# Loading the second round of scores into the staging space ahead of the first batch's gathers, in an argmax-gather-scatter kernel

## The chip, the cores and the metric

The kernel runs on one core of a Trainium2 chip. The metric is the device time of one execution in microseconds (us); lower is better. Before the change three runs took 908.44 to 910.4 us, with a median of 910.17 us.

## The reference

```python
def setup_inputs():
    B, S, H = (8, 2048, 2560)
    return {'scores': np.random.randn(B, S, S).astype(np.float32), 'values': np.random.randn(B, S, H).astype(np.float32)}

def reference(scores, values):
    best_j = np.argmax(scores, axis=2)
    b_idx = np.arange(B)[:, None]
    gathered = values[b_idx, best_j, :].copy()
    out = np.zeros_like(values)
    np.add.at(out, (b_idx, best_j, slice(None)), gathered)
    return out
```

For each of 8 batches, every one of the 2048 rows of scores picks the column with its maximum. Row j of the output is row j of the values times the number of score rows that picked j. So a values row that nobody picked becomes zeros, one that was picked once is copied, and one that was picked several times is multiplied by its count. With random scores a row is picked 0 times, once, or several times with chances of about 0.368, 0.368 and 0.264.

## The kernel before

**Scores.** `count_steps` (line 150) goes through the 16 tiles of a batch, 128 score rows each. A score load (line 160, queue of SyncE, called SP in the profile) brings two tiles at once: 128 partitions x 4096 numbers, 2 MiB, from 64 loads in all. This document numbers the loads 0 to 63 as the variable `x` does; batch 0 has loads 0 to 7, batch 1 loads 8 to 15. For each tile VectorE (DVE) runs MAX8 (line 168) and FIND_INDEX8 (line 169); every four tiles it makes one-hot matrices (lines 174 to 184), from which TensorE adds the counts of the batch into `cnt_ps` (line 187). After each tile the generator yields.

**Where the scores land.** There are ten places of 2 MiB. Seven are the buffers of the pool `spool` (`s_tile`). The other three lie in `vbig`, a tensor of six staging slots of 2560 columns (10,240 bytes per partition, one values row each) that the gathers use later. The test on line 155 sends loads 0, 1, 2 and 10, 11, 12 into `vbig`, at columns 0 to 4095, 4096 to 8191 and 8192 to 12287; all others go to `s_tile`. Loads 10, 11 and 12 belong to tiles 4 to 9 of batch 1. They overlay slots 0 to 4.

**Values.** `value_steps` (line 191) turns the counts of a batch into three kinds of transfers, all issued by GpSimd (POOL) as indirect DMAs whose index lists hold an out-of-range number where a row is to be skipped:

- a copy (`copy_once`, line 203, issued on line 33): rows that were picked once, from values to output directly, 16 per batch;
- a zero scatter (`scatter` of `zrow`, line 139): rows of zeros for the rows that nobody picked, 7 per batch;
- for the many-counted rows a gather (line 134) into a slot of `vbig`, a multiplication by the counts on ScalarE (ACT, line 280), and a scatter to the output (line 139), 5 of each per batch. The gathers take slots in turn (`stage`, line 145): batch 0 uses slots 0 to 4, batch 1 slots 5, 0, 1, 2, 3.

The index lists come from VectorE work between the yields: the scans (lines 212 to 228), the large one-hot compare `oh` (line 239), and, after two matmul groups (lines 258 and 261), the lists `many_i` and `zero_i` and the factors `many_c` (lines 268 to 272).

**What sets the order.** PE, DVE, ACT and SP run in the order in which the program is written (line 300). GpSimd's DMAs are placed by the scheduler, which keeps dependences. The framework derives waits from program order: whoever comes later in the program and touches a place that an earlier instruction reads or writes must wait for that one. The outer loop (line 302) runs the steps of batch b+1's counting and advances `value_steps` of batch b by one step after each tile. Batch 0 is the exception: on lines 309 to 311 its `value_steps` are run to their end before batch 1's counting begins. So in program order batch 0's gathers and scatters, which use slots 0 to 4, come before loads 10, 11 and 12, which overwrite these slots.

The end of the program (line 321) waits until all copies and zero scatters have landed.

Of the kernel before, what the change touches and what calls it, by code (L numbers as in the profile page):

```python
# [36 lines left out]
def kernel(  # L37
# [8 lines left out]
    _, _, H = values.shape  # L46
# [144 lines left out]
    def value_steps(b, cnt_ps):  # L191
# [98 lines left out]
                    copy_once(rest.pop(0))  # L290


        for part in (zeros, gathers) if b == 0 else (gathers, zeros):
            part()
        for k in range(MCAP):
            scatter(staged[k], mi[:, k:k + 1])
        yield
# [2 lines left out]
    with tc.manual_schedule(engines={ET.PE, ET.DVE, ET.Activation, ET.SP}):  # L300
        pending = iter(())
        for b in range(B):
            cnt_ps = psum_c.tile([P, NT], FP32)
            for _ in count_steps(b, cnt_ps):
                next(pending, None)
            for _ in pending:
                pass
            pending = value_steps(b, cnt_ps)
            if b == 0:
                for _ in pending:  # L310
                    pass
        for _ in pending:
            pass
        over = fin.tile([1, 2], FP32)
        nc.vector.tensor_single_scalar(out=over[:, 0:1], in_=totmax[0:1, 0:1], scalar=float(ZCAP * P), op=ALU.is_gt)
        nc.vector.tensor_single_scalar(out=over[:, 1:2], in_=totmax[0:1, 1:2], scalar=float(MCAP * P), op=ALU.is_gt)
        over_i = fin.tile([1, 1], INT32)
        nc.vector.tensor_tensor(out=over_i[:], in0=over[:, 0:1], in1=over[:, 1:2], op=ALU.add)
# [44 lines left out]
```

## Time and profile before

| | us |
|---|---|
| three runs, median (lowest to highest) | 910.17 (908.44 to 910.4) |
| the profiled execution, device time | 909.32 |
| its span, first to last instruction | 907.4 |
| VectorE busy | 687.8 |
| GpSimd busy (issuing DMAs) | 275.7 |
| ScalarE busy | 102.9 |
| TensorE busy | 18.0 |

The profile is one execution on the chip. A line of the timeline gives the start in us, the duration, the engine, the line of the program, the operation, what it writes and reads, how many, and in brackets how long the engine was idle before it and what ended that wait. A line of the waits gives who waited for whom: the total in us, how often, and the longest. A line of the stretches view gives for a piece of the span (from:to) its length, the busy time of PE, PEld, DVE, ACT and POOL with the number of instructions in brackets, the clock of TensorE, the mean busy share of the core's 16 DMA engines, and the GB/s that they moved. The first of the DMA queues, `q0`, is GpSimd's; `q1` is that of SP, with the score loads. In all 347.05 MB are moved.

### The profile page before, as it was taken

The numbers are of one execution on the slowest core, as the hardware profiler recorded it, in microseconds if no ns is written. First come the engines' busy times: TensorE is split into PE (matmuls) and PEld (weight loads), VectorE is DVE, ScalarE is ACT, GpSimd is POOL, SyncE is SP. The second block draws the span as 40 slices with busy tenths as digits, with TensorE's granted clock in tenths as the row PEclk, the third lists the DMA queues.
The fourth block names the chain that finished last, engine by engine and source line by source line (L and its number), as shares of the span: only waits on it lengthen the run. The fifth ranks groups of instructions, "written<-read, shape, count | busy, mean of one in ns | idle before, by whom it ended". The sixth has DMA issues, their size and how long they took to land.

```text
span 907.4 us, 2251 instructions
## 1 busy us (share of the span) xinstructions
PE 18.0 (2%) x400; PEld 16.9 (2%) x400; DVE 687.8 (76%) x741; ACT 102.9 (11%) x43; POOL 275.7 (30%) x275
## 2 busy tenths in 40 slices
PE   0000000000000000000000000000000000000000
PEld 0000000000000000000000000000000000000000
DVE  6999820499999999999999999999999994000000
ACT  2000005000023000032000320002200320400500
POOL 0001742000456012623015430064211753735600
DMA  9920899999779999999999999999999999999991
GB/s 381 428 116 12 260 401 424 373 428 381 286 304 417 426 426 429 427 426 424 429 427 424 429 427 426 427 427 426 428 429 418 423 425 423 423 424 421 424 399 53
DMA packets 47249, 347.05 MB, mean 382 GB/s; under 512 B 18279, under 2 KB 18279, under 8 KB 18279
## 3 DMA queue, kind: packets, MB, share of 16 engines
q0 software_dynamic: 38016, 212.67, 57.0%
q1 hardware_dynamic: 9216, 134.22, 35.1%
q14 instruction: 14, 0.11, 0.0%
q8 instruction: 3, 0.05, 0.0%
HBM read 354.42 MB, written 293.60 MB: 714 GB/s over the span
## 4 chain that ended last, share of the span: by engine, by line
DVE 68%; DMA 11%; POOL 9%; issue 7%; POOLq 0%; PE 0%; SPq 0%; DVEq 0%
DVE am L169 30%; DVE mx L168 28%; DMA out_dram<-vbig,many_i 9%; POOL out_dram L33 5%; POOL out_dram L139 3%; DVE oh L239 3%; DMA vbig<-in_scores_dram 2%; DVE oh_lo L178 2%; POOL vbig L134 1%; DVE lo L174 1%; DVE oh_hi L182 0%; DVE rz L247 0%; DVE hi L176 0%; DVE ez L243 0%; DVE rank L233 0%
## 5 line engine op out<-in xcount | busy, mean ns | idle before, releaser
L169 DVE FIND_INDEX8 am<-mx,s_tile 128x8 uint32<-128x2048 f32 x116 | 265.0, 2285 | 0.0
L168 DVE MAX8 mx<-s_tile 128x8 f32<-128x2048 f32 x116 | 264.3, 2278 | 0.0
L33 POOL DMA_INDIRECT out_dram<-in_values_dram,ones_i x128 | 134.7, 1052 | 228.6 <-DVE m L214 190.4
L280 ACT ACTIVATE vbig<-vbig,many_c 128x2560 f32<-128x2560 f32 x40 | 96.7, 2426 | 755.9 <-DMA vbig<-in_values_dram,many_i 748.6
L134 POOL DMA_INDIRECT vbig<-in_values_dram,many_i x40 | 42.1, 1052 | 228.3 <-DMA out_dram<-vbig,many_i 193.0
L139 POOL DMA_INDIRECT out_dram<-vbig,many_i x40 | 39.0, 976 | 110.6 <-ACT vbig L280 104.6
L168 DVE MAX8 mx<-vbig 128x8 f32<-128x2048 f32 x12 | 27.4, 2280 | 58.0 <-DMA vbig<-in_scores_dram 58.0
L139 POOL DMA_INDIRECT out_dram<-zrow,zero_i x56 | 58.5, 1045 | 17.1 <-issue 16.1
L239 DVE TENSOR_TENSOR oh<-lo,fill_f 128x4096 f16<-128x4096 uint32 x8 | 35.4, 4428 | 0.0
L169 DVE FIND_INDEX8 am<-mx,vbig 128x8 uint32<-128x2048 f32 x12 | 27.4, 2285 | 0.0
L178 DVE TENSOR_TENSOR oh_lo<-lo,lane_f 128x512 bf16<-128x512 uint32 x32 | 22.2, 694 | 0.4
L187 PE MATMUL cnt_ps<-oh_hi,oh_lo 128*128 128x16 bf16 x128 | 8.1, 174 | 622.9 <-DVE oh_hi L182 581.4
L187 PEld LDWEIGHTS <-oh_lo 128*128 128x128 bf16 x128 | 8.4, 105 | 622.6 <-DVE oh_lo L178 599.3
L169 DVE MATCH_VALUE_LOAD am<-mx,s_tile 128x8 f32 x116 | 10.7, 92 | 4.0
L182 DVE TENSOR_TENSOR oh_hi<-hi,lane_f 128x64 bf16<-128x64 uint32 x32 | 7.0, 219 | 0.0
L174 DVE TENSOR_SCALAR lo<-am 128x4 uint32<-128x4 uint32 x32 | 6.0, 186 | 1.1
L258 PE MATMUL m_ps<-rm,oh 128*128 128x16 f16 x128 | 4.7, 175 | 81.0 <-DVE rm L254 81.0
L176 DVE TENSOR_SCALAR hi<-am 128x4 uint32<-128x4 uint32 x32 | 5.7, 177 | 0.0
L258 PEld LDWEIGHTS <-oh 128*128 128x128 f16 x128 | 4.1, 105 | 81.6 <-DVE rm L254 74.8
L261 PE MATMUL z_ps<-rz,oh 128*128 128x16 f16 x128 | 4.6, 174 | 0.0
L261 PEld LDWEIGHTS <-oh 128*128 128x128 f16 x128 | 4.0, 104 | 0.0
L247 DVE TENSOR_TENSOR rz<-ez,row_f 128x256 f16<-128x256 f16 x8 | 3.4, 429 | 0.3
(52 smaller groups left out, 55.0 us busy)
## 6 DMA issues: line engine op xcount, KB each, us to landing
s_tile<-in_scores_dram SPq DMA_DIRECT2D x58, 2048.0 KB, 12.0
vbig<-in_scores_dram SPq DMA_DIRECT2D x6, 2048.0 KB, 9.1
out_dram<-in_values_dram,ones_i POOLq DMA_INDIRECT x128
out_dram<-zrow,zero_i POOLq DMA_INDIRECT x56
vbig<-in_values_dram,many_i POOLq DMA_INDIRECT x40
out_dram<-vbig,many_i POOLq DMA_INDIRECT x40
```

What stands on the lines that cost most here:

```text
L33: return eng.add_instruction(ins)
L134: nc.gpsimd.indirect_dma_start(out=v, out_offset=None, in_=values_flat[:, :], in_offset=bass.IndirectOffsetOnAxis(ap=idx, axis=0), bounds_ ...
L139: note(nc.gpsimd.indirect_dma_start(out=out_flat[:, :], out_offset=bass.IndirectOffsetOnAxis(ap=idx, axis=0), in_=v, in_offset=None, bound ...
L168: nc.vector.max(out=mx[:], in_=rows)
L169: nc.vector.max_index(out=am[:, g, :], in_max=mx[:], in_values=rows)
L174: nc.vector.tensor_single_scalar(out=lo[:], in_=am[:, :, 0], scalar=P - 1, op=ALU.bitwise_and)
L178: nc.vector.tensor_tensor(out=oh_lo[:], in0=lo[:].unsqueeze(2).to_broadcast([P, G, P]), in1=lane_f[:].unsqueeze(1).to_broadcast([P, G, P]) ...
L187: nc.tensor.matmul(out=cnt_ps[:], lhsT=oh_lo[:, g, :], rhs=oh_hi[:, g, :], start=(t == 0), stop=(t == NT - 1))
L239: nc.vector.tensor_tensor(out=oh[:], in0=lo[:].unsqueeze(2).to_broadcast([P, 2 * NT, P]), in1=fill_f[:].unsqueeze(1).to_broadcast([P, 2 * ...
L258: nc.tensor.matmul(out=m_ps[:], lhsT=oh[:, NT + t, :], rhs=rm[:, t, :, :].rearrange("p a k -> p (a k)"), start=(t == 0), stop=(t == NT - 1))
L261: nc.tensor.matmul(out=z_ps[:], lhsT=oh[:, t, :], rhs=rz[:, t, :], start=(t == 0), stop=(t == NT - 1))
L280: nc.scalar.activation(out=v, in_=v, func=mybir.ActivationFunctionType.Copy, bias=0.0, scale=mc[:, k:k + 1])
```

## The change

Batch 0's `value_steps` are no longer run to their end before batch 1's counting. Only their first four steps are: the last of these issues the zero scatters and then stops at the first of ten new yields. The other nine yields are passed one per tile of batch 1, and after tile 9 of batch 1 the gathers, the multiplications and the scatters of batch 0 follow. By then loads 10, 11 and 12 (and all loads up to those of tile 9) have been written down. So in program order these three loads now come before batch 0's gathers. Other batches keep their order of parts.

```diff
@@ -290,8 +290,15 @@ value_steps
-        for part in (zeros, gathers) if b == 0 else (gathers, zeros):
-            part()
+        if b == 0:
+            zeros()
+
+            for _ in range(10):
+                yield
+            gathers()
+        else:
+            gathers()
+            zeros()
         for k in range(MCAP):
             scatter(staged[k], mi[:, k:k + 1])
         yield
@@ -307,8 +314,8 @@ the outer loop
             pending = value_steps(b, cnt_ps)
             if b == 0:
-                for _ in pending:
-                    pass
+                for _ in range(4):
+                    next(pending)
```

SP's queue around loads 8 to 13, with what each waits for: names that begin with DMAHW are score loads, DMASW are GpSimd's DMAs. Before:

```order
L160 DMA s_tile<-in_scores_dram 128x4096 [waits DMAHW0_49]
L160 DMA s_tile<-in_scores_dram 128x4096 [waits DMAHW1_49]
L160 DMA vbig<-in_scores_dram 128x4096 [waits DMASW6_49,DMASW5_49,DMAHW2_49,DVE_49,Activation_49]
L160 DMA vbig<-in_scores_dram 128x4096 [waits DMASW7_49,DMASW0_49,DMAHW3_49,DVE_49,Activation_49]
L160 DMA vbig<-in_scores_dram 128x4096 [waits DMASW1_49,DMAHW4_49,DVE_49,Activation_49]
L160 DMA s_tile<-in_scores_dram 128x4096 [waits DMAHW5_49,DVE_49]
```

And now, at the same place of SP's queue:

```order
L160 DMA s_tile<-in_scores_dram 128x4096 [waits DMAHW0_49]
L160 DMA s_tile<-in_scores_dram 128x4096 [waits DMAHW1_49]
L160 DMA vbig<-in_scores_dram 128x4096 [waits DMAHW2_49,DVE_49]
L160 DMA vbig<-in_scores_dram 128x4096 [waits DMAHW3_49,DVE_49]
L160 DMA vbig<-in_scores_dram 128x4096 [waits DMAHW4_49,DVE_49]
L160 DMA s_tile<-in_scores_dram 128x4096 [waits DMAHW5_49,DVE_49]
```

The three loads keep their place in the queue; their waits for GpSimd's DMAs (batch 0's scatters) and for ScalarE are gone, and the waits for an earlier load and for VectorE stay.

GpSimd's queue from batch 0's last zero scatters to batch 1's gathers, as one piece of the difference (batch 0's five gathers, its five scatters, then batch 1's copies and gathers):

```order
 L139 DMA out_dram<-zrow,zero_i 16384x2560 x6
-L134 DMA vbig<-in_values_dram,many_i 128x2560 [waits DMAHW0_49]
-L134 DMA vbig<-in_values_dram,many_i 128x2560 [waits DMAHW1_49]
-L134 DMA vbig<-in_values_dram,many_i 128x2560
-L134 DMA vbig<-in_values_dram,many_i 128x2560 [waits DMAHW2_49]
-L134 DMA vbig<-in_values_dram,many_i 128x2560 [waits Activation_49]
+L134 DMA vbig<-in_values_dram,many_i 128x2560 [waits DMAHW2_49,DVE_49]
+L134 DMA vbig<-in_values_dram,many_i 128x2560 [waits DMAHW3_49,DVE_49]
+L134 DMA vbig<-in_values_dram,many_i 128x2560 [waits DVE_49]
+L134 DMA vbig<-in_values_dram,many_i 128x2560 [waits DMAHW4_49,DVE_49]
+L134 DMA vbig<-in_values_dram,many_i 128x2560 [waits DVE_49,Activation_49]
```

The gathers stand at the same place in GpSimd's queue, but each now waits for VectorE too, which must have read the scores of loads 10 to 12 from that slot. A little further on, where batch 1's transfers begin:

```order
-L33 DMA out_dram<-in_values_dram,ones_i 16384x2560 [waits landed0,DVE_49]
-L33 DMA out_dram<-in_values_dram,ones_i 16384x2560 x5
+L33 DMA out_dram<-in_values_dram,ones_i 16384x2560 [waits DVE_49]
+L33 DMA out_dram<-in_values_dram,ones_i 16384x2560 x3
 L134 DMA vbig<-in_values_dram,many_i 128x2560 [waits DMASW2_49,DVE_49]
```

Batch 1 has four copies ahead of its first gather now, where it had six, and the wait for batch 0's copies and zeros (`landed0`) has moved from here to the end of the program, where the other batches' stand.

## The prediction

> **What bounds the kernel now.** I read the page first: the span, and the GB/s that the DMA engines moved in 40 slices of 22.7 us.
>
> ```profile
> span 907.4 us, 2251 instructions
> GB/s 381 428 116 12 260 401 424 373 428 381 286 304 417 426 426 429 427 426 424 429 427 424 429 427 426 427 427 426 428 429 418 423 425 423 423 424 421 424 399 53
> ```
>
> The DMA engines run at one level, about 426 GB/s, for nearly the whole span. The exceptions are a hole in the third to fifth slice and a second, shallower one in the tenth to twelfth. A kernel that is otherwise held by its transfers gets shorter by what such holes are worth, so the question is who makes them. The waits name it:
>
> ```profile
> DVE mx L168 <- DMA vbig<-in_scores_dram: 58.0, 2, 52.1
> ```
>
> ```profile
> SPq L160 <- DMA out_dram<-vbig,many_i: 156.2, 3, 145.4
> ```
>
> VectorE waits once for 52.1 us, for a score load into `vbig`; and the SP queue sat 145.4 us before that load, waiting for scatters out of `vbig`. The timeline of SP shows the place:
>
> ```profile
> 0.75 1.33 SPq L160 DMA_DIRECT2D vbig<-in_scores_dram  x3
> 2.12 11.50 SPq L160 DMA_DIRECT2D s_tile<-in_scores_dram  x7
> 159.17 12.00 SPq L160 DMA_DIRECT2D vbig<-in_scores_dram  x3
> 171.28 84.47 SPq L160 DMA_DIRECT2D s_tile<-in_scores_dram  x12
> ```
>
> Ten loads are issued by 13.6 us, the eleventh (load 10) at 159.17. Everything behind it on SP waits too. GpSimd's timeline tells what it waits for (first copy of batch 0; first and last gather; first and last scatter; then batch 1's first copy and first gather):
>
> ```profile
> 87.77 1.12 POOL L33 DMA_INDIRECT out_dram<-in_values_dram,ones_i  x1 [85.81 <-DVE m L214]
> ...
> 121.85 1.04 POOL L134 DMA_INDIRECT vbig<-in_values_dram,many_i  x1 [0.30 <-issue]
> ...
> 127.09 0.99 POOL L134 DMA_INDIRECT vbig<-in_values_dram,many_i  x1 [0.30 <-issue]
> ...
> 144.69 1.00 POOL L139 DMA_INDIRECT out_dram<-vbig,many_i  x1 [16.61 <-ACT vbig L280]
> ...
> 156.61 0.96 POOL L139 DMA_INDIRECT out_dram<-vbig,many_i  x1 [1.35 <-ACT vbig L280]
> ...
> 234.43 0.98 POOL L33 DMA_INDIRECT out_dram<-in_values_dram,ones_i  x1 [76.85 <-DVE m L214]
> ...
> 257.00 1.04 POOL L134 DMA_INDIRECT vbig<-in_values_dram,many_i  x1 [11.48 <-DVE empty L270]
> ```
>
> Load 10 needs batch 0 counted (88 us), copied, zeroed, gathered, scaled and scattered. On VectorE:
>
> ```profile
> 8.43 2.29 DVE L168 MAX8 mx<-vbig 128x8 f32<-128x2048 f32 x1 [5.91 <-DMA vbig<-in_scores_dram]
> ...
> 82.91 2.28 DVE L169 FIND_INDEX8 am<-mx,s_tile 128x8 uint32<-128x2048 f32 x1
> ...
> 98.61 2.28 DVE L168 MAX8 mx<-s_tile 128x8 f32<-128x2048 f32 x1
> ...
> 170.38 2.29 DVE L168 MAX8 mx<-vbig 128x8 f32<-128x2048 f32 x1 [52.08 <-DMA vbig<-in_scores_dram]
> ...
> 228.77 2.29 DVE L168 MAX8 mx<-s_tile 128x8 f32<-128x2048 f32 x1
> ...
> 759.75 0.15 DVE L318 TENSOR_TENSOR over_i<-over 1x1 int32<-1x1 f32 x1
> ```
>
> Batch 0's 16 tiles take 8.43 to 85.2, or 9.6 us per load of two tiles. From 170.38 to 228.77 lie twelve tiles, 9.73 us per load. VectorE has its last result at 759.75, but the span goes on to 907.4. The stretches view shows why:
>
> ```profile
> 10.00:50.00 40.00, 0.51 (x8) 0.52 (x8) 39.62 (x35) 0.00 (x0) 0.00 (x0) 1.00 1.01 431
> 50.00:86.00 36.00, 0.25 (x4) 0.26 (x4) 35.65 (x29) 0.00 (x0) 0.00 (x0) 1.00 0.04 17
> 86.00:95.00 9.00, 0.45 (x6) 0.50 (x7) 8.38 (x24) 0.00 (x0) 6.62 (x3) 1.00 0.17 48
> 95.00:112.00 17.00, 1.00 (x32) 0.90 (x31) 14.04 (x15) 0.00 (x0) 13.04 (x14) 1.00 0.96 311
> 112.00:160.00 48.00, 0.26 (x4) 0.26 (x4) 6.21 (x8) 12.03 (x5) 17.31 (x18) 1.00 1.01 410
> 160.00:172.00 12.00, 0.00 (x0) 0.00 (x0) 1.62 (x1) 0.00 (x0) 0.00 (x0) 1.00 0.83 323
> 172.00:214.00 42.00, 0.51 (x8) 0.53 (x8) 41.62 (x36) 0.00 (x0) 0.00 (x0) 1.00 1.00 428
> 214.00:234.00 20.00, 0.25 (x4) 0.26 (x4) 19.69 (x20) 0.00 (x0) 0.00 (x0) 1.00 0.83 319
> 234.00:260.00 26.00, 1.49 (x38) 1.32 (x38) 25.59 (x40) 0.00 (x0) 11.96 (x9) 1.00 0.67 239
> 260.00:300.00 40.00, 0.51 (x8) 0.52 (x8) 39.65 (x33) 12.14 (x5) 24.21 (x25) 1.00 1.01 420
> 300.00:760.00 460.00, 12.75 (x288) 11.86 (x288) 452.83 (x499) 48.34 (x20) 142.16 (x138) 1.00 1.01 426
> 760.00:880.00 120.00, 0.00 (x0) 0.00 (x0) 0.00 (x0) 24.16 (x10) 59.06 (x60) 1.00 1.02 423
> 880.00:907.40 27.40, 0.00 (x0) 0.00 (x0) 0.00 (x0) 0.00 (x0) 0.00 (x0) 1.00 0.23 97
> ```
>
> From 260 to 880 the DMA engines are full (share 1.01), through VectorE's end at 760. After 760 they still carry 120 x 423 and 27.4 x 97 GB/s-us, 53.4 MB, about two batches of values. So the bound is the DMA engines from 260 on; VectorE never waits there, it runs ahead of a backlog. What decides the end is how many bytes were moved before the saturated part begins.
>
> **The change part by part.** *The holes, added up.* From 50 to 260 the rows above move 0.6 + 0.4 + 5.3 + 19.7 + 3.9 + 18.0 + 6.4 + 6.2 = 60.5 MB. At 426 GB/s this is 142 us of work in 210 us: **68 us** are lost, by stretch 34.6 (50:86), 8.0, 4.6, 1.8, 2.9, 0, 5.0 and 11.4 (234:260).
>
> That rate is weighed against a rule. The row 300:760 holds 426 GB/s for 460 us. The Trainium skill, page HBM Reference, section Specifications (TRN2), gives an effective share of about 358 GB/s per core, and about 425 for a core that streams alone. By 358 the 60.5 MB would be 169 us of work, the loss 41, and the time below some 27 us higher; the trace agrees with the page's other figure.
>
> *What is removed.* Load 10 now waits only for load 2 and for VectorE to be done with load 0, which is at 8.43 + 9.6 = 18 us; loads 11 and 12 at 28 and 37. All three are issued while the first ten still move (to about 51.4: the row 50:86 has 0.6 MB left, 1.4 us). A load is 2.097 MB, 4.92 us at 426. So 10 to 12 land by 66.2. Loads 13 to 17 are issued as VectorE frees loads 3 to 7: at 46.8, 56.4, 66.0, 75.6, 85.2. They land by 71.1, 76.0, 80.9, 85.9 and, for the last, about 93: the first load of all came 7.7 us after its issue (0.75 to 8.43), 2.8 more than its bytes need. VectorE's stall of 52.1 goes too: at 118.3 load 10 has long been there. All its later work comes 52.1 earlier, batch 1's first copy at 182.3 for 234.43, its gathers at 204.9 for 257.00, its last result at 707.7.
>
> *What is kept of the holes.*
> - 50:86: 34.6 before; the transfers now follow one another almost without a gap. I keep 1.5 (0 to 3).
> - 86:95: 8.0 before; load 17 gives 4.9 of the 9 us, the first copy 1.0 as before. I keep 3 (0 to 8.0).
> - 95:112: only copies, 311 GB/s; load 18 comes at 108.3 (98.61 + 9.7). 4.6 before; I keep 3.5 (2 to 4.6).
> - 112:160, 1.8 before: I keep 1, since a load every 9.7 us joins. 160:172: nothing, load 10 no longer starts from an empty queue.
> - 214:260, 16.4 before, falls at 162 to 208 now. GpSimd's transfers are these:
>
> ```profile
> q0 software_dynamic: 38016, 212.67, 57.0%
> ```
>
> 212.67 MB over 8 batches is 26.6 MB each, 62 us at 426. From 95 to 182 there are 61 us of batch 0's transfers, eight loads (18 to 25, issued 108 to 176) of 4.92 = 39, and 4.5 of slow copying: 105 us of work in 87. So the engines stay full, and about 18 us are left over at 182. From 182 to 205 four copies (0.48 MB each, 6 us at the row's 311 GB/s) and load 26 come in, with the start of load 27 about 12 us: 30 for 23. That covers it, but not by much, and the last scatters wait for ScalarE one by one. I keep 4, between 0 and the 11.4 of before, nearer the full end because a backlog exists now and did not then.
>
> Kept: 1.5 + 3 + 3.5 + 1 + 4 = 13. **Gain 68 - 13 = 55 us.**
>
> *What is added.* Batch 0's gathers wait for VectorE to finish loads 10 to 12. VectorE is done with load 10 at 118.3 + 9.7 = 128, 11 at 138, 12 at 147.5; GpSimd gets to the first gather at 121.85 and holds there. Its gathers go at 128, 138, 138, 147.5, 147.5 instead of 121.85 to 127.09. Behind them on GpSimd are only batch 0's scatters and then batch 1's copies, not ready until 182.3. The scatters came 17.6 to 29.5 us after the last gather was issued (144.69 and 156.61 against 127.09), so now by about 177. Cost on the path: 0, while batch 1's copies are the cover; without it, 20.4 us (147.5 - 127.09) at most. Two copies fewer ahead of batch 1's gathers is counted above; `landed0` at the end costs nothing, batch 0 having landed long before. Ten more yields issue nothing.
>
> **The sum.** Profiled execution 909.32 - 55 = 854.3. The runs' median is 0.85 above that execution, so **855**.
>
> **The rivals.**
> 1. *The second hole comes back.* Between batch 1's copies and gathers the engines run dry as before (11.4 for 4), and the load into 86:95 starts late (8.0 for 3). Kept 13 + 7.4 + 5 = 25, gain 43: 867; with the first alone 862.5. For it: only four copies now stand ahead of the gathers. Against: 18 us of backlog at 182. Chance 0.12.
> 2. *VectorE paces the end.* If the tail behind VectorE's last result (907.4 - 759.75 = 147.6) were a fixed chain, the gain would be the stall alone, 52.1: 858. Against it: the tail is 53.4 MB at full rate. Chance 0.1, within the range.
> 3. *Memory itself is the limit, no change.* The page counts
>
> ```profile
> DMA packets 47249, 347.05 MB, mean 382 GB/s; under 512 B 18279, under 2 KB 18279, under 8 KB 18279
> ...
> HBM read 354.42 MB, written 293.60 MB: 714 GB/s over the span
> ```
>
> If the memory could give no more than this mean, filling holes would only slow the rest, and 648 MB would again take 907 us. Against it: the mean includes 36 us at 17 GB/s, and 347.05 MB moved stand for 648 in memory, so the 426 of 300:760 is 795 already. The Trainium skill, HBM Reference, same section, gives about 716 GB/s per memory domain, by which 648 MB need 905 us, no gain; the 795 speaks against it as a cap on this count. Chance 0.03.
> 4. *Slower: GpSimd stands still behind the late gathers.* If batch 0's scatters landed after batch 1's gathers want their slots (204.9), GpSimd, in order, would hold those and all copies and zeros behind them. It costs when the last scatter lands after 205, and makes the kernel slower when it lands after about 262 (57 us later, more than the gain); at 270 the time would be 918 or so. How long gather and scatter take with full engines is seen near the end (a gather, its scatter, the gather that waits for that to land):
>
> ```profile
> 739.78 1.04 POOL L134 DMA_INDIRECT vbig<-in_values_dram,many_i  x1 [0.30 <-issue]
> ...
> 789.83 0.98 POOL L139 DMA_INDIRECT out_dram<-vbig,many_i  x1 [0.30 <-issue]
> ...
> 822.21 1.02 POOL L134 DMA_INDIRECT vbig<-in_values_dram,many_i  x1 [17.36 <-DMA out_dram<-vbig,many_i]
> ```
>
> 50 and 32 us: 147.5 + 82 is 230, still 32 us short of 262, and the loads would fill the engines meanwhile. Chance 0.02.
>
> That load 10 isn't freed is excluded by SP's order: no wait for a scatter is left on it.
>
> **How the numbers follow.** My forecast has 0.73, its own range 848 (kept 6, the 55 becoming 62) to 862 (kept 20). Rival 2 lies inside; of rival 1 the range takes most, up to 866. So 848 to 866. About 0.2% is what a measurement of this kernel can tell from no change: faster 0.95, same 0.03, slower 0.02.
>
> **What would show it.** SP issues loads 10 to 12 before 40 us; VectorE has no wait above 5 us after its start and ends near 708; the stretch 50 to 86 runs above 400 GB/s; GpSimd waits for VectorE before batch 0's gathers until 147; from 112 on the engines are full except for a dent below 5 us near 190 to 205. The prediction is wrong if that dent is as deep as before, if VectorE waits for scores again, or if the saturated level sinks below 420 GB/s.

## The result and the profile after

| | before | after |
|---|---|---|
| runs, median (lowest to highest), us | 910.09 (908.44 to 910.4) | 860.15 (860.01 to 860.97) |
| the profiled execution, us | 909.32 | 860.97 |
| its span, us | 907.4 | 859.2 |

Before has one run more here than the three given ahead, so its median moves from 910.17 to 910.09. The ratio of the times is 0.9457, with a 95% interval of 0.944 to 0.9473: the kernel is 49.9 us faster. 855 had been predicted, with a range of 848 to 866.

The page of the changed kernel gives the span and the GB/s in 40 slices, of 21.5 us each:

```profile
span 859.2 us, 2246 instructions
GB/s 378 427 427 427 289 390 428 419 413 248 428 419 426 427 426 429 426 429 424 427 426 428 425 427 428 429 426 425 428 424 420 424 426 413 425 425 421 425 370 35
```

The deep hole is gone: the second to fourth slices are at 427. Two dents remain: the fifth slice (289) and the tenth (248). VectorE's waits, and SP's timeline:

```profile
DVE mx L168 <- DMA vbig<-in_scores_dram: 6.2, 1, 6.2
```

```profile
0.75 1.33 SPq L160 DMA_DIRECT2D vbig<-in_scores_dram  x3
2.12 11.81 SPq L160 DMA_DIRECT2D s_tile<-in_scores_dram  x7
18.57 19.23 SPq L160 DMA_DIRECT2D vbig<-in_scores_dram  x3
...
108.13 9.51 SPq L160 DMA_DIRECT2D s_tile<-in_scores_dram  x2
...
156.49 0.33 SPq L160 DMA_DIRECT2D s_tile<-in_scores_dram  x1
...
166.74 9.51 SPq L160 DMA_DIRECT2D s_tile<-in_scores_dram  x2
...
187.86 0.33 SPq L160 DMA_DIRECT2D s_tile<-in_scores_dram  x1
```

VectorE waits for scores at the start alone, for the first load. Loads 10 to 12 are issued from 18.57 to 37.8. The rows further down matter for the error below: loads 18 and 19 from 108.13, load 20 only at 156.49, 21 and 22 from 166.74, 23 at 187.86. GpSimd's first gather and its last scatter of batch 0, then batch 1's first copy and first gather:

```profile
128.05 1.04 POOL L134 DMA_INDIRECT vbig<-in_values_dram,many_i  x1 [6.22 <-DMA s_tile<-in_scores_dram]
...
170.17 0.96 POOL L139 DMA_INDIRECT out_dram<-vbig,many_i  x1 [3.52 <-ACT vbig L280]
182.61 0.98 POOL L33 DMA_INDIRECT out_dram<-in_values_dram,ones_i  x1 [11.48 <-DVE m L214]
...
205.19 1.04 POOL L134 DMA_INDIRECT vbig<-in_values_dram,many_i  x1 [17.77 <-DVE empty L270]
```

The first gather is later (128.05 for 121.85), as the added wait says. The view names a score load as what ended its wait, but it lies behind VectorE's last read of load 10, which in VectorE's timeline starts at 125.50 and takes 2.29 us. Batch 1's copies are not held up by this: GpSimd is idle for 11.48 us before them. The stretches view (last two columns: share of the DMA engines, GB/s) answers the table of before:

```profile
50.00:86.00 36.00, 0.26 (x4) 0.27 (x4) 35.65 (x30) 0.00 (x0) 0.00 (x0) 1.00 1.00 423
86.00:95.00 9.00, 0.45 (x6) 0.49 (x7) 8.38 (x23) 0.00 (x0) 6.34 (x2) 1.00 0.78 285
95.00:112.00 17.00, 1.00 (x32) 0.90 (x31) 14.13 (x16) 0.00 (x0) 13.01 (x14) 1.00 0.94 309
112.00:182.00 70.00, 1.01 (x16) 1.04 (x16) 69.25 (x62) 12.14 (x5) 17.57 (x18) 1.00 1.01 418
182.00:190.00 8.00, 0.21 (x2) 0.13 (x2) 7.83 (x18) 0.00 (x0) 3.89 (x4) 1.00 1.00 394
190.00:202.00 12.00, 1.02 (x32) 0.93 (x32) 11.86 (x12) 0.00 (x0) 0.00 (x0) 1.00 0.57 228
202.00:205.00 3.00, 0.26 (x4) 0.26 (x4) 2.93 (x8) 0.00 (x0) 0.00 (x0) 1.00 0.38 71
205.00:210.00 5.00, 0.00 (x0) 0.00 (x0) 4.93 (x6) 0.00 (x0) 3.90 (x4) 1.00 0.86 349
210.00:260.00 50.00, 0.52 (x8) 0.53 (x8) 49.59 (x39) 12.14 (x5) 24.68 (x26) 1.00 1.01 424
260.00:700.00 440.00, 11.75 (x256) 10.96 (x256) 433.98 (x476) 48.45 (x20) 142.05 (x138) 1.00 1.01 426
```

A stretch of length L that moved r GB/s lost L x (426 - r) / 426. The rows give 0.3, 3.0, 4.7, 1.3, then 0.6 + 5.6 + 2.5 + 0.9 = 9.6 from 182 to 210, and 0.2: together 19 us, where the kernel before lost 68. The difference, 49, is the 48.2 us between the two spans within 1 us. VectorE's last result comes at

```profile
707.95 0.15 DVE L325 TENSOR_TENSOR over_i<-over 1x1 int32<-1x1 f32 x1
```

### The profile page after: what moved, and what is told of

The parts are those of the page before. It is cut to its first block, busy times and chain, and to the rows that moved or that the text cites. A ratio compares the mean times of both kernels' runs of the same rounds, so it can differ in the third digit from the quotient of the medians.

```text
span 859.2 us, 2246 instructions
## 1 busy us (share of the span) xinstructions
PE 18.0 (2%) x400; PEld 17.0 (2%) x400; DVE 687.9 (80%) x741; ACT 103.2 (12%) x43; POOL 271.7 (32%) x275
## 3 DMA queue, kind: packets, MB, share of 16 engines
HBM read 354.42 MB, written 293.60 MB: 754 GB/s over the span
## 4 chain that ended last, share of the span: by engine, by line
DVE 69%; DMA 9%; POOL 7%; issue 5%; another core or an unknown queue 4%; PE 0%; POOLq 0%
DVE am L169 31%; DVE mx L168 29%; DMA out_dram<-vbig,many_i 8%; DVE oh L239 3%; POOL out_dram L33 3%; POOL out_dram L139 3%; DVE oh_lo L178 2%; POOL vbig L134 1%; DMA vbig<-in_scores_dram 1%; DVE lo L174 1%; DVE oh_hi L182 0%; DVE rz L247 0%; DVE hi L176 0%; DVE ez L243 0%
## 5 line engine op out<-in xcount | busy, mean ns | idle before, releaser
L33 POOL DMA_INDIRECT out_dram<-in_values_dram,ones_i x128 | 130.1, 1016 | 155.3 <-DVE m L214 117.0
L139 POOL DMA_INDIRECT out_dram<-vbig,many_i x40 | 41.4, 1035 | 105.8 <-ACT vbig L280 101.1
```

The source lines that it names most:

```text
L33: return eng.add_instruction(ins)
L139: note(nc.gpsimd.indirect_dma_start(out=out_flat[:, :], out_offset=bass.IndirectOffsetOnAxis(ap=idx, axis=0), in_=v, in_offset=None, bound ...
```

## The experiments

Theory A, that of the prediction: the DMA engines set the end, and what decides is how much they have moved before the part from about 210 us on, in which they stay full until near the end. Theory B (rival 2 of the prediction): VectorE's end plus a fixed tail sets it. Times are medians; the ratio to the kernel before, measured together with it, and the interval of this ratio stand beside each. In this section *batch 1's early copies* are those ahead of its first gather.

### Does the dent cost what the sum says? More early copies

```diff
-        first = NT if b == 0 else 4
+        first = NT if b < 2 else 4
```

> The changed kernel with all 16 copies of batch 1 (instead of 4) ahead of its first gather. Theory A (the end is set by how many bytes the DMA engines have moved; the changed kernel runs dry from 190 to 205 us because nothing is queued there): twelve more copies of 0.48 MB are about 13 us of work, the dent of some 9.6 us closes, 851 us (849 to 854), while VectorE's last result stays at 708. Theory B (VectorE's end plus a fixed tail sets the time): VectorE's end doesn't move, so 860.

Measured: **852.98 us** (0.9381, 0.9369 to 0.9394), 7.2 us faster than the changed kernel, within A's bounds. The stretches from 182 on:

```profile
182.00:190.00 8.00, 0.22 (x2) 0.13 (x2) 7.86 (x17) 0.00 (x0) 6.17 (x6) 1.00 1.02 392
190.00:202.00 12.00, 1.02 (x32) 0.93 (x32) 11.86 (x12) 0.00 (x0) 9.86 (x8) 1.00 1.00 403
202.00:205.00 3.00, 0.26 (x4) 0.26 (x4) 2.87 (x9) 0.00 (x0) 2.39 (x3) 1.00 0.99 345
205.00:210.00 5.00, 0.00 (x0) 0.00 (x0) 4.97 (x6) 0.00 (x0) 3.78 (x5) 1.00 1.04 352
```

The dent is filled to 392 to 403 GB/s; these rows still lose 0.6 + 0.6 + 0.6 + 0.9 = 2.7 us, 6.9 less than the 9.6 of the changed kernel and close to the gain of 7.2. VectorE's last result:

```profile
711.09 0.15 DVE L325 TENSOR_TENSOR over_i<-over 1x1 int32<-1x1 f32 x1
```

It came 3 us *later* than in the changed kernel (VectorE waited 3.31 us on line 270 shortly before it), while the end came 8.7 us of span earlier. That excludes B.

### Fewer early copies

```diff
-        first = NT if b == 0 else 4
+        first = NT if b == 0 else 0 if b == 1 else 4
```

> The changed kernel with none of batch 1's copies (instead of 4) ahead of its first gather. Theory A (bytes moved by the DMA engines before the saturated part): four copies of 0.48 MB, 1.13 us each at 426 GB/s, leave the stretch 182 to 205 us, the dent gets 4.5 us deeper, 864.7 us (862 to 867). Theory B (VectorE's end plus a fixed tail): 860.

Measured: **859.64 us** (0.945, 0.9437 to 0.9463), neither slower than the changed kernel nor the 864.7 expected. The edit did something that its expectation doesn't say: there are only twelve places for copies beside the gathers and the zero scatters, so this kernel leaves four of batch 1's copies out and its output lacks their rows. It has 4.5 us less to move and a dent that is deeper by about as much. The time of a kernel with less work cannot judge the theory, so the same was run with the four copies after the zero scatters:

```diff
+        while rest:
+            copy_once(rest.pop(0))
         for k in range(MCAP):
             scatter(staged[k], mi[:, k:k + 1])
```

> The changed kernel with none of batch 1's copies ahead of its first gather (instead of 4), and all 16 of them issued: five between the gathers, seven between the zero scatters, the last four after these. The run before this one of that kind had left these four copies out and took 859.64 us. Theory A (bytes moved before the saturated part begins at 205 us): the same dry stretch, and now four copies of 1.13 us more to move after it, 864.2 us (863 to 866). Rival (the four copies ahead of the gathers matter for nothing): 860.

Measured: **862.43 us** (0.9484, 0.947 to 0.9497). 2.3 us slower than the changed kernel, about half of what A expects, just below its 863 to 866, and clear of the rival's 860. Its trace shows the deeper dent, and a second difference:

```profile
190.00:202.00 12.00, 1.02 (x32) 0.93 (x32) 11.83 (x15) 0.00 (x0) 0.00 (x0) 1.00 0.19 78
...
202.00:205.00 3.00, 0.25 (x4) 0.26 (x4) 2.93 (x8) 0.00 (x0) 1.91 (x2) 1.00 0.93 284
```

```profile
202.78 1.04 POOL L134 DMA_INDIRECT vbig<-in_values_dram,many_i  x1 [30.87 <-DVE empty L270]
```

The engines fall to 78 GB/s as they should, but the gather that ends the dent comes at 202.78, 2.4 us sooner than in the changed kernel. Most of this comes from batch 0: between the two instructions of line 270 VectorE waited 1.8 us in the changed kernel and doesn't here. That wait is in the traces of before, of the changed kernel and of some experiments, and absent from others; the hardware section takes it up. With 2.4 us added back, which is an estimate and was not measured, the run would stand at 864.8, near the 864.2 expected.

### Is VectorE's end on the path?

```diff
                 nc.vector.max_index(out=am[:, g, :], in_max=mx[:], in_values=rows)
+                if b == 4 and u < 4:
+                    again = small.tile([P, 8], FP32, name="again")
+                    nc.vector.max(out=again[:], in_=rows)
```

> The changed kernel with eight more MAX8 of 2.28 us on VectorE, whose results are not used, in the first eight tiles of batch 4: 18 us of extra VectorE work in the saturated part. Theory A (the DMA engines set the end from about 205 us on, VectorE runs ahead of a backlog): VectorE's last result comes at 726, the time stays 860 (859 to 863). Theory B (VectorE paces the end): 878.

Measured: **860.25 us** (0.9458, 0.9443 to 0.9472), the time of the changed kernel. VectorE's last result:

```profile
727.86 0.15 DVE L328 TENSOR_TENSOR over_i<-over 1x1 int32<-1x1 f32 x1
```

It moved by 20 us and the end by none. So the 51.8 us by which the change ended VectorE's work sooner (707.95 for 759.75) are not themselves the gain.

### One of the three loads left behind

```diff
-            for _ in range(10):
+            for _ in range(8):
                 yield
```

> The changed kernel with eight yields instead of ten: batch 0's gathers come after tile 7 in program order, so loads 10 and 11 precede them and load 12 comes after and waits for two scatters. Theory A (what counts is how long SP's queue is blocked, and with it every load behind): loads 12 to 17 aren't there by 95 us, VectorE stalls about 40 us before tile 8 of batch 1, most of the gain is lost, 897 us (885 to 905). Rival (the gain comes load by load, a third for each of the three): 877.

Measured: **892.48 us** (0.9813, 0.9798 to 0.9828). Two loads of three in front keep 17 of 50 us; a third for each load would have kept 33. SP's waits and VectorE's:

```profile
SPq L160 <- DMA out_dram<-vbig,many_i: 137.7, 1, 137.7
```

```profile
DVE mx L168 <- DMA vbig<-in_scores_dram: 41.2, 2, 35.1
```

SP is blocked for 137.7 us by load 12 alone, as it was for 145.4 by load 10 before, and VectorE stalls for 35.1 (52.1 before). From 50 to 86 most of the hole is back:

```profile
50.00:86.00 36.00, 0.26 (x4) 0.27 (x4) 35.65 (x29) 0.00 (x0) 0.00 (x0) 1.00 0.31 133
```

The row loses 24.8 us, where before lost 34.6: the difference, 9.8, is two loads of 4.92. What counts is the first load that waits, since every later one queues behind it. The time came out 4.5 us below the 897 expected, with a stall of 35 for the estimated 40.

### Without the second round in the staging space

The kernel before, its order untouched, with loads 10 to 12 in `s_tile`:

```diff
-            if x < 2 * (NX + NB) and x % (NX + NB) < NX:
+            if x < NX:
```

> The kernel before, with loads 10 to 12 in buffers of s_tile instead of the staging space; the order of gathers and loads stays as before. Theory A (the loss of before is the block of SP's queue behind batch 0's scatters; the additional early places matter little): load 10 waits for VectorE's load 3 (46.8 us), no stall, but only loads up to 14 are there by 95 us instead of 17, some 15 us of DMA work missing in 50 to 95, of which 9 to 10 come back in 182 to 205; 865 us (862 to 870). Rival (the early loads into the staging space are what brings the gain): with them gone most of it goes, 890 or more.

Measured: **864.9 us** (0.9513, 0.95 to 0.9526). All but 4.8 us of the change's gain is had without its reordering, by not using the staging space a second time. The stretches show the exchange:

```profile
50.00:86.00 36.00, 0.25 (x4) 0.26 (x4) 35.65 (x29) 0.00 (x0) 0.00 (x0) 1.00 0.66 249
...
190.00:202.00 12.00, 1.02 (x32) 0.93 (x32) 11.83 (x15) 6.03 (x3) 3.33 (x3) 1.00 0.96 407
```

The first loses 15.0 us (0.3 in the changed kernel), for three loads that have no place yet. Everything behind them moves later: batch 0's last scatter is issued at 202.13, where the changed kernel had it at 170.17, and the engines have this work from 190 to 202 (407 for 228 GB/s). From 182 to 210 this kernel loses 1.3 us where the changed one loses 9.6. So of the 14.7 us that the early loads brought, some 8 were borrowed from the dent. As a control, the same kernel with sixteen early copies:

```diff
-        first = NT if b == 0 else 4
+        first = NT if b < 2 else 4
```

> The kernel before with loads 10 to 12 in s_tile buffers (864.9 us) and with all 16 copies of batch 1 ahead of its first gather. Theory A (early copies gain only because they fill a stretch in which the engines run dry): without the second round in the staging space the engines move 402 GB/s from 190 to 205 already, so about 1 us is to be had, 864 us (862.5 to 866). Rival (early copies are better by themselves, by the 7 us that they brought to the changed kernel): 858.

Measured: **865.07 us** (0.9517, 0.9503 to 0.953), no gain. The early copies that brought 7.2 us to the changed kernel bring nothing where there is no dent, as A expects; the 858 of the rival is excluded.

### How far SP can load ahead

```diff
-    NB = 7
+    NB = 6
-            for _ in range(10):
+            for _ in range(8):
```

> The changed kernel with six s_tile buffers instead of seven (the second round in the staging space is then loads 9 to 11, tiles 2 to 7 of batch 1, and eight yields put the gathers behind it). Theory A (how far SP can load ahead sets what the DMA engines can be given before 205 us: ten places until the second round is over, then only the s_tile buffers): one load of 4.9 us less by 205 us, 865 us (863 to 868), VectorE without a stall. Rival (the depth doesn't matter as long as VectorE doesn't stall): 860.

Measured: **862.2 us** (0.9479, 0.9466 to 0.9492), slower than the changed kernel by 2.1, not by the 5 expected, and below the range of 863 to 868. The hole of one load is there (4.9 us of 36 by this row):

```profile
50.00:86.00 36.00, 0.26 (x4) 0.26 (x4) 35.65 (x29) 0.00 (x0) 0.00 (x0) 1.00 0.89 368
```

VectorE never stalls, so the rival, which expects 860, is excluded only by these 2 us. This kernel too lacks batch 0's wait on line 270: its first gather of batch 1 comes at 202.68 for 205.19. With 2.5 added, again an estimate, it would be 864.7.

### A version that beats both

All copies of batch 1 early, and batch 0's copies spread between its zero scatters and gathers as in the other batches:

```diff
-        first = NT if b == 0 else 4
+        first = NT if b == 1 else 4
```

> The changed kernel with all 16 copies of batch 1 ahead of its first gather, and in batch 0 only four copies ahead of the lists, the other twelve placed between zero scatters and gathers as in later batches. Theory A (bytes moved before the saturated part): the dent of 190 to 205 us closes (9 us), and between 95 and 112, where copies alone moved 309 GB/s, zeros and copies together fill the engines (3 to 4 us more); 848 us (845 to 851). Theory B (VectorE's end plus a fixed tail): 860. If copies alone cost nothing more than copies between zeros, 851.

Measured: **850.62 us** (0.9362, 0.9348 to 0.9377), the lowest median here and 9.5 us below the changed kernel. Against the sixteen early copies alone (852.98, ratio 0.9369 to 0.9394) the 2.4 us are not clear of the noise: the intervals overlap, and the five runs go from 849.93 to 853.26.

```profile
99.00:112.00 13.00, 0.00 (x0) 0.00 (x0) 12.90 (x9) 0.00 (x0) 9.96 (x11) 1.00 1.00 390
...
182.00:205.00 23.00, 1.28 (x36) 1.19 (x36) 22.67 (x30) 0.00 (x0) 18.43 (x16) 1.00 1.00 382
```

The engines move 390 GB/s from 99 to 112, where the changed kernel moves 335; over the whole stretch from 95 to 112 it is 349 for 309. The expectation gave 848 if this filled the engines and 851 if copies alone cost nothing more; the time lies nearer to the second. This kernel also lacks the wait on line 270, which the one with sixteen early copies has. So that spreading batch 0's copies brings anything isn't shown.

## Why the prediction was right, and where it was off

- **The bound and the mechanism** held. The gain is what the holes lost before less what they lose now, 68.1 - 19 = 49. VectorE's extra work cost nothing, and the time moved with the fill of the dent while VectorE's end went the other way.
- **The removed wait**: loads 10 to 12 were due at 18, 28 and 37 and went from 18.57 to 37.8; VectorE's end was due at 707.7 and came at 707.95.
- **50:86** kept 0.3 for 1.5; **86:95** 3.0 for 3; **95:112** 4.7 for 3.5, just over the upper bound of 4.6: load 18 was issued at 108.13, as foreseen, and the row moved 309 GB/s for the 311 of before; **112 to 182** 1.3 for 1.
- **214:260 of before, now 182 to 210**, is the term that was mis-sized: 9.6 for 4. Of the signs named, "a dent below 5 us near 190 to 205" is the one that did not come: these 15 us lost 8.1. The step that failed is the ledger behind it, "eight loads (18 to 25, issued 108 to 176)". SP issued five in that time. Ten places for loads exist only until the second round in the staging space is over; from load 20 on there are the seven buffers of `s_tile`, so load 20 waits until VectorE is done with load 13, and not with load 10. It went at 156.49, 39 us after load 19. SP's waits from 95 to 215 have this as the longest (line 176 follows right on VectorE's last read of load 13, which ends at 156.47):

```profile
SPq L160 <- DVE hi L176: 63.7, 3, 39.0
```

Three loads of 4.92 us, 14.8 us, were missing from the 18 us of backlog on which the 4 rested. The code said so (line 155); the ledger didn't read it. With five loads the same ledger has 105 - 14.8 = 90 us of work in 87, 3 us left over at 182, and with some 12 more by 205 that is 15 for 23: a dent of 8 us.
- So most of **rival 1** is what happened, in its first part: it had 862.5 for a dent of 11.4 us, and a chance of 0.12 with its second part, a late load into 86:95, which did not happen. With a dent of 8 us the prediction's sum would have kept 17 and given 859.
- **Rival 2** is excluded by two runs, the sixteen early copies and the eight MAX8 more. The tail behind VectorE's end grew from 147.6 to 151.2 us.
- **Rival 3**: the page after counts

```profile
HBM read 354.42 MB, written 293.60 MB: 754 GB/s over the span
```

The same megabytes in less time, so the 714 GB/s of before were no limit of the memory. The Trainium skill, page HBM Reference, section Specifications (TRN2), gives about 716 GB/s per domain; on this count the trace lies above it, as a mean over the whole span. What the count takes in isn't known: it has 293.60 MB written, while the output is 16,384 rows of 10,240 bytes, 167.8 MB, each written once.
- **Rival 4** did not happen: batch 0's last scatter was issued at 170.17, ahead of the 177 estimated, and GpSimd then stood idle for 11.48 us until batch 1's first copy was ready. So the added wait held up nothing on GpSimd.

## What to carry to other kernels

Where several loads share one in-order queue, the first of them that must wait holds all: look for a load whose buffer overlays something that is written late, and price it by what everything behind it would have moved. Before filling a hole with early work, make a ledger of which work is left for the next thin stretch, load by load with the buffer that each waits for; part of what is gained early is only borrowed. Where the transfers are the bound, move work that is ready sooner into the stretches in which the queues run dry, and don't read a shorter wait of a compute engine as the gain.

## What the runs showed of the hardware

- Indirect copies from memory to memory, with some 47 of 128 rows of 10 KB to move in each, gave 309 GB/s from 95 to 112 in the changed kernel (one load beside them from 108) and 311 in the kernel before (none beside them), at a DMA share of 0.94 and 0.96, where the mixed traffic later moves 426 at 1.01. GpSimd issues one every 1.27 us there, and 0.48 MB in 1.27 us are 378 GB/s at most, by estimate; how much of the low rate is the pace of the issues wasn't separated.
- One issue of batch 0's copies took 5.22 us, and those behind it 0.97 to 1.01. VectorE's large compare on line 239 ran at the same time:

```profile
89.44 4.42 DVE L239 TENSOR_TENSOR oh<-lo,fill_f 128x4096 f16<-128x4096 uint32 x1
```

```profile
89.50 5.22 POOL L33 DMA_INDIRECT out_dram<-in_values_dram,ones_i  x1 [0.30 <-issue]
```

The kernel before has the same pair at 89 us, and another at 240 (4.70 us beside 4.42). It falls in the stretch from 86 to 95, the dent of the fifth slice. That the compare holds up the issue is what the coincidence suggests; no run moved one away from the other.
- Between batch 0's two instructions on line 270 VectorE waited 1.8 to 1.9 us in some runs, none of it explained by TensorE's records. In the changed kernel:

```profile
98.45 0.18 DVE L270 TENSOR_SCALAR empty<-z_ps 128x16 f32<-128x16 f32 x1 [1.84 <-remote]
```

With six buffers the same instruction starts at 96.27 with no wait. The experiments ran on two chips, and the wait goes with the chip: the four on one (sixteen early copies, the kernel with four copies left out, eight MAX8 more, one load left behind) all have it, and the five on the other have none. The two kernels without early copies, which differ only in four copies of batch 1, fall on different sides. No kernel has a trace from both chips, so chip and edit aren't fully separated, and which chip the changed kernel's own trace is from isn't on record. Where a few microseconds decide, the wait is as large as the effect: the 2 to 5 us between the changed kernel and an experiment without the wait are uncertain by about 2.5 us.
